# Second-round convolutions one per two steps, and weight sums begun eight steps later, in the up stage of a one-core hybrid block

## The chip, the core and the metric

One core of a Trainium2 chip runs the whole program. The metric is the device time in microseconds of one execution; the number compared is the median of several runs. Engines are called as the profile calls them: PE multiplies matrices (PEld is its weight load), DVE and ACT work elementwise, POOL and SP mostly issue DMAs.

## The reference

A transformer block for 256 tokens of width 2048: three kinds of attention merged by gates, and then a feed-forward part. The change touches only the feed-forward part, which in the reference is

```
h2 = rms_norm(x, g_ffn)
u = causal_depthwise_conv(h2 @ w_up, conv_w, conv_b)      # 3 taps along the tokens
u_gate, u_val = split(u, 2)                               # 5632 columns each
x = x + (silu(u_gate) * u_val) @ w_down
```

All in float32. The kernel gets that precision from cheaper matmuls by splitting each operand into a rounded part (hi) and the rest (lo) and adding the products.

## The kernel before, in words

**Up stage.** The 5632 gate columns and 5632 value columns are cut into 44 tiles of 128 each. The loop over `f0` takes four tiles at a time, first of the gate half (`s` = 0) and then of the value half (`s` = 1). One such pass is called a round here: 11 values of `f0` times two, 22 rounds. The first round is (f0 = 0, s = 0), the second (0, 1), the third (4, 0), the fourth (4, 1). A round goes over the 2048 inputs in 8 **steps** of two k-tiles; 176 steps in all, numbered here from 0, so the second round is steps 8 to 15 and the third 16 to 23.

A step needs 512 KB of `w_up`. `piece` (lines 134 to 146) issues the load on SP, rounds it on ACT into `hi_u` (L141), and subtracts on DVE to get `lo_u` (L142). Then PE runs 8 pairs of matmuls: L1168 multiplies `hi_u` with 512 columns (the tokens' hi and lo parts side by side), L1169 multiplies `lo_u` with the 256 hi columns. There are four buffers each of `raw`, `hi` and `lo`, so a step's operands can be ready a few steps ahead.

**Work beside the matmuls.** After its matmuls each step calls `tick()`, which advances two kinds of generators by one:

- `background` holds two streams of `weight_sums`. Every 8 steps each of them loads a piece of `w_down` (two DMAs of 256 KB on SP, L258), forms sums of its blocks on DVE (L267, L268, L269), and six steps later stores them to DRAM (L272), from where the down stage reads them. `delay` is the number of ticks that a stream waits before its first piece: `14 + 2 * i` here. The staging tiles are `pre_d…`, the stored ones `kept_d…`.
- `later(...)` puts a generator in a queue of which at most two (`WINDOW`) are active. A finished round queues four `conv`: copy and add from PSUM (L1110 on ACT, L1111 on DVE), scale by the row norm `rbc` (L1120 DVE), then three taps (L1125 ACT, L1126 and L1127 DVE). For the gate half follows SiLU (L1129 ACT). For the value half follow the product with the gate (L1133 DVE) and the split of the result into `aT` (L175 ACT, L176 DVE). A `conv` does all of this in one tick.

The first round is special. Its results are ready before `rbc` is: `rbc` is computed from the sum of squares, stored and read back by two POOL DMAs (L1044, L1045). So `first_convs` empties the PSUM banks at once, waits three ticks, and applies one convolution per tick after that.

The loads, the splits of `piece` and the sums keep their order in the program; the convolutions' instructions are placed among them by a scheduler that follows dependencies. Each engine then executes its own list strictly in that order, so an instruction of a convolution that stands ahead of a `lo_u` split on DVE delays that split.

At f0 = 40 the streams must have taken all their pieces; what they have left to issue is drained there.

Of the kernel before, what the change touches and what calls it, by code (L numbers as in the profile page):

```python
# [9 lines left out]
F32 = mybir.dt.float32  # L10
# [5 lines left out]
P = 128  # L16
# [25 lines left out]
def hybrid_block(  # L42
# [54 lines left out]
    def later(gen):  # L97
        waiting.append(gen)
# [57 lines left out]
    def product(x_of, w, nk, n0, n, name):  # L156

        ps = [bank(f"{name}_{t}") for t in range(NT)]
        wv = w.rearrange("(k p) n -> p k n", p=P)
        for k in range(0, nk, 2):  # L160
            a = min(2, nk - k)
            wh, wl = piece(wv[:, k : k + a, n0 : n0 + n], a, n, f"{name}_{k}")
            order = [(j, t) for j in range(a) for t in range(NT)]
            if k + a == nk:
                order.sort(key=lambda jt: jt[1])
            for j, t in order:
                xk = x_of(k + j)
                xs_ = xk[:, t * P : (t + 1) * P], xk[:, S + t * P : S + (t + 1) * P]
                three(ps[t][:, :n], *xs_, (wh[:, j], wl[:, j]), k + j == 0, k + j == nk - 1)
            tick()  # L170
        return ps
# [558 lines left out]
    ps = proj(C_MQ, MEM_W, "mq")  # L730
# [36 lines left out]
    for c in range(3):  # L767
        ps = proj(c * 512, 512, f"f{c}")
# [7 lines left out]
    ps = proj(1536, 512, "f3")  # L776
# [3 lines left out]
    ps = proj(2048, 262, "f4")  # L780
# [74 lines left out]
    for c in range(3):  # L855
        ps = proj(C_SB + c * 512, 512, f"s{c}")
# [51 lines left out]
    ps = proj(C_SB + 1536, 512, "s3")  # L908
# [4 lines left out]
    ps = proj(C_SB + 2048, 256, "s4")  # L913
# [39 lines left out]
    for m in range(2):  # L953
        gate = []
        for b, plan in enumerate(g_plans[m]):
# [40 lines left out]
            if not plan:  # L996
                biases()
                for n in range(2):
                    ps = proj(c0 + n * 512, 512, f"g{n}_{b}")
# [12 lines left out]
        for n in range(2):  # L1012
            acc = gate[branches[0][3]][n]
            for i, (w, k0, nk, b) in enumerate(branches):
                ps = product(lambda k: oT[:, k0 + k], w[0], nk, (2 * m + n) * 512, 512, f"b{2 * m + n}_{b}")
# [61 lines left out]
    ff = ctx.enter_context(tc.tile_pool(name="ff", bufs=1))  # L1077
# [4 lines left out]
    for i in range(2):  # L1082
        background.append(
            weight_sums(
                lambda name, i=i: ff.tile([P, 1024], F32, tag=f"end{i}", bufs=1, name=name), 8, 6, delay=14 + 2 * i
            )
        )

# [20 lines left out]
    def out_of(ps, dst):  # L1109
        nc.scalar.copy(dst, ps[:, S:])  # L1110
        nc.vector.tensor_tensor(dst, dst, ps[:, :S], ALU.add)  # L1111
        return dst
# [4 lines left out]
    def taken(cr, y, f, s):  # L1117
        ct = s * FT + f
        u = pads[f % 2]
        ins = nc.vector.tensor_tensor(u[:, 2:], cr, rbc, ALU.mult)  # L1120
        if y is not None:
            in_order(ins)
        y = y_tile(f, s) if y is None else y
        tap = lambda j: taps[:, j, ct : ct + 1]
        nc.scalar.activation(y, u[:, 2:], AF.Identity, scale=tap(2), bias=tap(3))  # L1125
        nc.vector.scalar_tensor_tensor(y, u[:, 1 : S + 1], tap(1), y, ALU.mult, ALU.add)  # L1126
        nc.vector.scalar_tensor_tensor(y, u[:, 0:S], tap(0), y, ALU.mult, ALU.add)  # L1127
        if s == 0:
            nc.scalar.activation(y, y, AF.Silu)  # L1129
            ys[f] = y  # L1130
        else:
            g = ys.pop(f)
            nc.vector.tensor_tensor(g, g, y, ALU.mult)  # L1133
            split_to(a_pair(f // 2)[:, f % 2], g)

    def conv(ps, f, s):
        taken(out_of(ps, cp.tile([P, S], F32, tag="cr", bufs=2, name=f"cr_{f}_{s}")), None, f, s)
        return
        yield

    def first_convs(ps):
        kept = []
        padded()
        for f in range(4):
            kept.append(out_of(ps[f], y_tile(f, 0)))
            if f % 2:
                yield
        yield 3
        for f in range(4):
            taken(kept[f], kept[f], f, 0)  # L1150
            yield

    for f0 in range(0, FT, 4):
        if f0 == FA:
            assert not halves
            for g in background:
                deque(g, 0)
            background.clear()
        for s in range(2):
            ps = [bank(f"u{f0 + i}_{s}") for i in range(4)]  # L1160
            c0 = s * D_FF + f0 * P
            for k in range(0, KT, 2):
                hi, lo = piece(upv[:, k : k + 2, c0 : c0 + 512], 2, 512, f"u{f0}_{s}_{k}")
                for j in range(2):
                    first, last = k + j == 0, k + j == KT - 1
                    for i in range(4):
                        c = slice(i * P, (i + 1) * P)
                        nc.tensor.matmul(ps[i], lhsT=hi[:, j, c], rhs=hT(k + j), start=first, stop=False)  # L1168
                        nc.tensor.matmul(  # L1169
                            ps[i][:, :S], lhsT=lo[:, j, c], rhs=hT(k + j)[:, :S], start=False, stop=last  # L1170
                        )
                tick()
            if f0 + s == 0:
                later(first_convs(ps))
                continue
            for i in range(4):
                later(conv(ps[i], f0 + i, s))
# [90 lines left out]
```

## Time and profile before

| quantity | value |
|---|---|
| three runs | 1467.82, 1469.42, 1476.87 us |
| median | 1469.42 us |
| the profiled execution's own time | 1476.86 us |
| its span (first to last instruction) | 1475.1 us |
| PE busy | 1469.3 us (100%) |
| DVE busy | 1193.8 us (81%) |
| ACT busy | 839.8 us (57%) |
| matmuls of the up stage, L1168 and L1169 | 2816 |

The profiled execution is the slowest of the three. What lies around its span is 1476.86 − 1475.1 = 1.8 us. A matmul's duration in the rows overlaps with the next one's, so PE's pace has to be read from the distance between two starts and not from a mean duration; "PE busy 100%" only says that there is hardly a moment without a matmul in flight.

### The profile page before, as it was taken

What the parts mean: (1) busy time and instruction counts of PE and PEld (TensorE: products, weight loads), DVE (VectorE), ACT (ScalarE), POOL (GpSimd) and SP (SyncE); (2) the same over time, 40 slices, a digit from 0 to 9 for tenths busy, and PEclk for the clock granted to TensorE, in tenths of its full rate; (3) what the DMA queues carried; (4) which work ended last, traced back from release to release, by engine and by line L of the source; (5) the groups of instructions that cost most, each with busy time, mean ns of one, the idle gap of its engine ahead of it and who ended that gap; (6) DMA issues with size and microseconds to landing.
All of it is one profiled execution on the core that took longest, in us unless ns stands there. A gap on an engine that the chain in (4) does not pass through costs nothing.

```text
span 1475.1 us, 20662 instructions
## 1 busy us (share of the span) xinstructions
PE 1469.3 (100%) x7335; PEld 1240.1 (84%) x7335; DVE 1193.8 (81%) x1816; ACT 839.8 (57%) x1194; POOL 21.8 (1%) x48
## 2 busy tenths in 40 slices
PE   9999999999999999999999999999999999999998
PEld 7888888888888888888888888888888888888887
DVE  5777676777588899897888889888888877997877
ACT  6755454464364455546666656656556555674664
POOL 0000000021000000000000000000000000000000
PEclk9999999999999999999999999999999999999999
DMA  9686787687868576878778999889888866798795
GB/s 299 200 278 193 221 281 215 186 264 226 248 201 275 165 231 204 275 255 277 244 182 274 306 284 286 271 267 288 278 281 282 260 186 199 242 317 269 252 347 213
DMA packets 205606, 369.55 MB, mean 251 GB/s; under 512 B 13578, under 2 KB 82078, under 8 KB 205246
## 3 DMA queue, kind: packets, MB, share of 16 engines
q1 hardware_dynamic: 204094, 365.99, 78.6%
q10 hardware_dynamic: 1328, 2.11, 0.4%
q8 instruction: 57, 0.93, 0.2%
q14 instruction: 47, 0.39, 0.1%
q0 software_dynamic: 80, 0.13, 0.0%
HBM read 335.67 MB, written 32.51 MB: 250 GB/s over the span
## 4 chain that ended last, share of the span: by engine, by line
PE 98%; DVE 1%; ACT 0%; issue 0%; POOL 0%; POOLq 0%; DVEq 0%
PE u L1168 22%; PE u L1169 11%; PE xd L288 4%; PE xd L286 4%; PE xd L287 4%; PE xg L287 3%; PE xg L286 3%; PE xg L288 3%; PE f L288 2%; PE f L287 2%; PE f L286 2%; PE s L286 2%; PE s L288 2%; PE s L287 2%; PE g L286 2%; PE g L288 2%
## 5 line engine op out<-in xcount | busy, mean ns | idle before, releaser
L1168 PE MATMUL u<-hT,hi_u 128*128 128x512 f32 x1232 | 435.6, 398 | 0.0
L1169 PE MATMUL u<-hT,lo_u 128*128 128x256 f32 x1232 | 345.6, 281 | 0.5 <-DVE lo_u L142 0.5
L1168 PEld LDWEIGHTS u<-hT,hi_u 128*128 128x128 f32 x1232 | 231.5, 188 | 57.3
L142 DVE TENSOR_TENSOR lo_u<-raw_u,hi_u 128x1024 fp32r<-128x1024 f32 x176 | 215.3, 1223 | 72.8 <-ACT hi_u L141 70.9
L141 ACT CAST hi_u<-raw_u 128x1024 fp32r<-128x1024 f32 x176 | 184.8, 1051 | 150.2 <-PE u L1168 122.2
L1169 PEld LDWEIGHTS u<-hT,lo_u 128*128 128x128 f32 x1232 | 232.6, 189 | 0.9 <-DVE lo_u L142 0.9
L281 DVE TENSOR_TENSOR lo_d<-raw_d,hi_d 128x1024 fp32r<-128x1024 f32 x88 | 106.8, 1223 | 20.7 <-ACT hi_d L280 18.0
L280 ACT CAST hi_d<-raw_d 128x1024 fp32r<-128x1024 f32 x88 | 92.0, 1054 | 48.0 <-PE xd L287 23.0
L280 ACT CAST hi_g<-raw_g 128x1024 fp32r<-128x1024 f32 (+1 forms) x64 | 61.7, 973 | 37.4 <-PE xg L287 14.2
L281 DVE TENSOR_TENSOR lo_g<-raw_g,hi_g 128x1024 fp32r<-128x1024 f32 (+1 forms) x64 | 71.0, 1119 | 4.3 <-ACT hi_g L280 4.3
L141 ACT CAST hi_f<-raw_f 128x1024 fp32r<-128x1024 f32 (+1 forms) x40 | 38.6, 968 | 51.9 <-PE f L287 47.2
L142 DVE TENSOR_TENSOR lo_f<-raw_f,hi_f 128x1024 fp32r<-128x1024 f32 (+1 forms) x40 | 44.7, 1119 | 27.9 <-ACT hi_f L141 26.0
L286 PE MATMUL xd<-hi_d,aT 128*128 128x512 f32 x170 | 66.2, 389 | 0.0
L288 PE MATMUL xd<-lo_d,aT 128*128 128x512 f32 x170 | 66.2, 389 | 0.0
L287 PE MATMUL xd<-hi_d,aT 128*128 128x512 f32 x170 | 66.1, 389 | 0.0
L142 DVE TENSOR_TENSOR lo_s<-raw_s,hi_s 128x1024 fp32r<-128x1024 f32 (+1 forms) x40 | 44.7, 1117 | 24.9 <-ACT hi_s L141 23.0
L141 ACT CAST hi_s<-raw_s 128x1024 fp32r<-128x1024 f32 (+1 forms) x40 | 38.5, 962 | 43.7 <-PE s L287 27.7
L1168 PE MATMUL u<-hT_rest,hi_u 128*128 128x512 f32 x176 | 63.1, 398 | 0.0
L142 DVE TENSOR_TENSOR lo_g<-raw_g,hi_g 128x1024 fp32r<-128x1024 f32 x32 | 39.3, 1233 | 23.0 <-ACT hi_g L141 22.5
L1125 ACT ACTIVATE y<-u,taps 128x256 f32<-128x256 f32 x88 | 49.6, 597 | 13.8 <-DVE u L1120 13.8
L141 ACT CAST hi_b<-raw_b 128x1024 fp32r<-128x1024 f32 x32 | 33.4, 1053 | 41.1 <-PE b L287 15.9
L141 ACT CAST hi_g<-raw_g 128x1024 fp32r<-128x1024 f32 x32 | 33.6, 1052 | 37.3 <-PE g L287 34.7
(482 smaller groups left out, 3537.8 us busy)
## 6 DMA issues: line engine op xcount, KB each, us to landing
raw_u<-in_w_up_dram SPq DMA_DIRECT2D x176, 512.0 KB, 4.9
raw_g<-in_w_in_dram SPq DMA_DIRECT2D x96, 512.0 KB, 4.5
raw_d<-in_w_down_dram SPq DMA_DIRECT2D x66, 512.0 KB, 5.4
pre_d<-in_w_down_dram SPq DMA_DIRECT2D x88, 256.0 KB, 4.9
kept_d<-pre_d SPq DMA_DIRECT2D x44, 512.0 KB, 5.8
raw_f<-in_w_in_dram SPq DMA_DIRECT2D x32, 512.0 KB, 4.7
raw_s<-in_w_in_dram SPq DMA_DIRECT2D x32, 512.0 KB, 4.1
raw_o<-in_w_out_dram SPq DMA_DIRECT2D x25, 512.0 KB, 5.6
```

Of the source, the lines that this page charges most:

```text
L141: pin(nc.scalar.copy(hi[:, :m], raw[:, :m]))
L142: pin(nc.vector.tensor_tensor(lo[:, :m], raw[:, :m], hi[:, :m].bitcast(F32), ALU.subtract))
L280: nc.scalar.copy(hi[:, :n], src)
L281: nc.vector.tensor_tensor(lo[:, :n], src, hi[:, :n].bitcast(F32), ALU.subtract)
L286: fix(nc.tensor.matmul(o, lhsT=ah, rhs=w[0], start=first, stop=False))
L287: fix(nc.tensor.matmul(o, lhsT=al, rhs=w[0], start=False, stop=False))
L288: fix(nc.tensor.matmul(o, lhsT=ah, rhs=w[1], start=False, stop=last))
L1125: nc.scalar.activation(y, u[:, 2:], AF.Identity, scale=tap(2), bias=tap(3))
L1168: nc.tensor.matmul(ps[i], lhsT=hi[:, j, c], rhs=hT(k + j), start=first, stop=False)
L1169: nc.tensor.matmul(ps[i][:, :S], lhsT=lo[:, j, c], rhs=hT(k + j)[:, :S], start=False, stop=last)
```

## The change

The streams of weight sums in the up stage wait 22 and 24 steps in place of 14 and 16. And the second round's four convolutions are issued by one generator: nothing in its first tick, then one whole convolution (the `deque` runs it to its end), a tick without one, the next convolution, and so on. Before, up to two were issued in one tick.

```diff
-                lambda name, i=i: ff.tile([P, 1024], F32, tag=f"end{i}", bufs=1, name=name), 8, 6, delay=14 + 2 * i
+                lambda name, i=i: ff.tile([P, 1024], F32, tag=f"end{i}", bufs=1, name=name), 8, 6, delay=22 + 2 * i
...
+    def second_convs(ps):
+        yield
+        for f in range(4):
+            deque(conv(ps[f], f, 1), 0)
+            yield 1
...
-            if f0 + s == 0:
-                later(first_convs(ps))
+            if f0 == 0:
+                later((first_convs, second_convs)[s](ps))
                 continue
```

How this moves instructions is seen best on DVE in the third round. In the names, `lo_u4_0_6` is the lo part for f0 = 4, s = 0 and k-tile 6 (step 19; k-tile 2j is the round's step j). `cr_1_1` and `y_1_1` belong to the convolution of tile 1 of the value half, `y_1_0` to that of the gate half. Before, these are the last 12 rows up to and with the split for step 19; between the split for step 18, `lo_u4_0_4`, and the first of them stand two more:

```order
L1120 TENSOR_TENSOR u_0_6980<-cr_0_1_7204,rbc_5953 128x256
L1127 SCALAR_TENSOR_TENSOR y_3_0_7015<-u_1_6982,taps_110,y_3_0_7015 128x256
L1111 TENSOR_TENSOR cr_1_1_7242<-cr_1_1_7242,u1_1_6955 128x256
L1126 SCALAR_TENSOR_TENSOR y_0_1_7208<-u_0_6980,taps_110,y_0_1_7208 128x256
L1120 TENSOR_TENSOR u_1_6982<-cr_1_1_7242,rbc_5953 128x256
L1127 SCALAR_TENSOR_TENSOR y_0_1_7208<-u_0_6980,taps_110,y_0_1_7208 128x256
L1111 TENSOR_TENSOR cr_2_1_7275<-cr_2_1_7275,u2_1_6956 128x256
L1133 TENSOR_TENSOR y_0_0_6984<-y_0_0_6984,y_0_1_7208 128x256
L1126 SCALAR_TENSOR_TENSOR y_1_1_7246<-u_1_6982,taps_110,y_1_1_7246 128x256
L1120 TENSOR_TENSOR u_0_6980<-cr_2_1_7275,rbc_5953 128x256
L1127 SCALAR_TENSOR_TENSOR y_1_1_7246<-u_1_6982,taps_110,y_1_1_7246 128x256
L142 TENSOR_TENSOR lo_u4_0_6_7288<-raw_u4_0_6_7286,hi_u4_0_6_7287 128x1024
```

With the change, these are the rows behind the split for step 18, up to the split for step 20:

```order
L1126 SCALAR_TENSOR_TENSOR y_3_0_7015<-u_1_6982,taps_110,y_3_0_7015 128x256
L1111 TENSOR_TENSOR cr_0_1_7218<-cr_0_1_7218,u0_1_6954 128x256
L1127 SCALAR_TENSOR_TENSOR y_3_0_7015<-u_1_6982,taps_110,y_3_0_7015 128x256
L1120 TENSOR_TENSOR u_0_6980<-cr_0_1_7218,rbc_5953 128x256
L1111 TENSOR_TENSOR cr_1_1_7273<-cr_1_1_7273,u1_1_6955 128x256
L142 TENSOR_TENSOR lo_u4_0_6_7253<-raw_u4_0_6_7251,hi_u4_0_6_7252 128x1024
L1126 SCALAR_TENSOR_TENSOR y_0_1_7222<-u_0_6980,taps_110,y_0_1_7222 128x256
L1120 TENSOR_TENSOR u_1_6982<-cr_1_1_7273,rbc_5953 128x256
L1127 SCALAR_TENSOR_TENSOR y_0_1_7222<-u_0_6980,taps_110,y_0_1_7222 128x256
L1111 TENSOR_TENSOR cr_2_1_7328<-cr_2_1_7328,u2_1_6956 128x256
L1133 TENSOR_TENSOR y_0_0_6984<-y_0_0_6984,y_0_1_7222 128x256
L142 TENSOR_TENSOR lo_u4_0_8_7286<-raw_u4_0_8_7284,hi_u4_0_8_7285 128x1024
```

Thirteen instructions stood between the splits for steps 18 and 19, and eight between those for 19 and 20; now there are five and five, and the rest comes between later splits.

The second place is DVE at the end of the second round, from the split for step 14 to that for step 15. Before:

```order
L142 TENSOR_TENSOR lo_u0_1_12_7108<-raw_u0_1_12_7106,hi_u0_1_12_7107 128x1024
L267 TENSOR_TENSOR pre_d0_4_1_7128<-pre_d0_4_1_7128 128x512
L268 TENSOR_TENSOR pre_d0_4_1_7128<-pre_d0_4_1_7128 128x256
L269 TENSOR_TENSOR pre_d0_4_1_7128<-pre_d0_4_1_7128 128x256
L1120 TENSOR_TENSOR u_0_6980<-y_0_0_6984,rbc_5953 128x256
L142 TENSOR_TENSOR lo_u0_1_14_7141<-raw_u0_1_14_7139,hi_u0_1_14_7140 128x1024
```

With the change:

```order
L142 TENSOR_TENSOR lo_u0_1_12_7108<-raw_u0_1_12_7106,hi_u0_1_12_7107 128x1024
L1120 TENSOR_TENSOR u_0_6980<-y_0_0_6984,rbc_5953 128x256
L1126 SCALAR_TENSOR_TENSOR y_0_0_6984<-u_0_6980,taps_110,y_0_0_6984 128x256
L1127 SCALAR_TENSOR_TENSOR y_0_0_6984<-u_0_6980,taps_110,y_0_0_6984 128x256
L142 TENSOR_TENSOR lo_u0_1_14_7135<-raw_u0_1_14_7133,hi_u0_1_14_7134 128x1024
```

The three sums are gone from here, and the first convolution's product with `rbc`, with both taps that follow it, now stands directly behind the split for step 14 and ahead of the split for step 15.

The third place is SP's list at the other end of the stage, where the streams are drained. With the change:

```order
L258 DMA pre_d1_12_1_11362<-in_w_down_dram 128x2x256 x2
L272 DMA kept_d1_12_11186<-pre_d1_12_0_11187 512x1x256
L140 DMA raw_u36_1_14_11369<-in_w_up_dram 128x2x512
L140 DMA raw_u40_0_0_11396<-in_w_up_dram 128x2x512
L140 DMA raw_u40_0_2_11440<-in_w_up_dram 128x2x512
L140 DMA raw_u40_0_4_11484<-in_w_up_dram 128x2x512
L272 DMA kept_d1_12_11186<-pre_d1_12_1_11362 512x1x256
L140 DMA raw_u40_0_6_11506<-in_w_up_dram 128x2x512
```

Before, the last store stood in front of `raw_u36_1_10`, one round earlier:

```order
L140 DMA raw_u36_1_8_11303<-in_w_up_dram 128x2x512
L272 DMA kept_d1_12_10962<-pre_d1_12_1_11146 512x1x256
L140 DMA raw_u36_1_10_11326<-in_w_up_dram 128x2x512
L140 DMA raw_u36_1_12_11348<-in_w_up_dram 128x2x512
L140 DMA raw_u36_1_14_11370<-in_w_up_dram 128x2x512
```

Everything of the streams has moved by one round, so that the last store, which went out among the loads of the round (36, 1), now stands among those of (40, 0).

## The prediction

> **What bounds the kernel now.** I read the page first, then who PE waited for, then the starts of PE's matmuls in the up stage, and last the DVE rows ahead of the one wait there.
>
> ```profile
> span 1475.1 us, 20662 instructions
> PE 1469.3 (100%) x7335; PEld 1240.1 (84%) x7335; DVE 1193.8 (81%) x1816; ACT 839.8 (57%) x1194; POOL 21.8 (1%) x48
> ...
> PE 98%; DVE 1%; ACT 0%; issue 0%; POOL 0%; POOLq 0%; DVEq 0%
> ```
>
> PE is 98% of the chain that ended last. In PE's list of waits the up stage has one entry:
>
> ```profile
> PE spare L91 <- DVE qscale L487: 1.2, 1, 1.2
> PE u L1169 <- DVE lo_u L142: 0.5, 1, 0.5
> PE r L895 <- DVE ls L891: 0.2, 1, 0.2
> ```
>
> So the change, which moves only DVE, ACT and SP work, can remove one wait, and add others; nothing else of it is on the path. In the timeline of PE the place is this (start, duration, instruction):
>
> ```profile
> 804.63 0.28 PE L1169 MATMUL u<-hT,lo_u 128*128 128x256 f32 x1
> 804.75 0.39 PE L1168 MATMUL u<-hT,hi_u 128*128 128x512 f32 x1
> 805.68 0.39 PE L1169 MATMUL u<-hT,lo_u 128*128 128x256 f32 x1 [0.55 <-DVE lo_u L142]
> 805.91 0.39 PE L1168 MATMUL u<-hT,hi_u 128*128 128x512 f32 x1
> ```
>
> 804.75 is the start of step 20 (third round, k-tile 8). Its `hi_u` is there; its `lo_u` comes 0.7 us too late: the second matmul starts 0.93 us after the first, where 0.23 us is usual.
>
> More is lost behind it. The next rows are the up stage before, at and behind the wait and its last 15 full steps, restricted to L1168 (length, then busy time and count on PE and on PEld, granted clock, DMA share and GB/s), and one row of the down stage with all engines:
>
> ```profile
> 760.38:804.75 44.37, 44.37 (x130) 24.00 (x129) 1.00 0.85 244
> 804.75:808.38 3.63, 2.86 (x10) 1.50 (x9) 1.00 0.43 96
> 808.38:1243.69 435.31, 435.31 (x1234) 231.51 (x1233) 1.00 0.85 268
> 1201.29:1243.69 42.40, 42.40 (x122) 22.55 (x121) 1.00 0.63 186
> ...
> 1250.00:1450.00 200.00, 200.00 (x884) 165.66 (x883) 170.60 (x234) 125.98 (x160) 0.00 (x0) 1.00 0.87 286
> ```
>
> The stretches were cut at starts of L1168, so their true counts are two lower than shown: 128 pairs (16 steps) in the first, 1232 (154 steps) in the third. That is 44.37 / 16 = **2.773 us a step before the wait** and 435.31 / 154 = **2.827 us a step behind it**, 0.0535 us more, through to the end of the stage. The clock is 1.00 in all rows, and in the down stage a matmul of 512 columns starts every 200 / 884 = 0.226 us, as beside the wait (0.23). So it isn't PE's clock. Nor is it the weight sums or the DMA: the last steps have no sums and a DMA share of 0.63, and keep 42.40 / 15 = 2.827 us. The pace behaves like something that PE falls into at an interruption, and keeps. The stage has two more such points:
>
> ```profile
> 747.44 0.39 PE L1168 MATMUL u<-hT,hi_u 128*128 128x512 f32 x1
> ...
> 750.25 0.40 PE L1168 MATMUL u<-hT,hi_u 128*128 128x512 f32 x1
> ...
> 753.08 0.38 PE L195 MATMUL hT<-ident,xres_again 128*128 128x128 f32 x2
> ...
> 757.60 0.39 PE L1168 MATMUL u<-hT,hi_u 128*128 128x512 f32 x1
> ```
>
> Step 0 takes 2.81 us, behind the change of stage; step 3 begins at 757.60, behind the transposes of `hT`, and from there to 804.75 are 17 steps of 2.774. What inside PE sets the pace the profile doesn't show.
>
> **What the change removes.** The wait comes from DVE. These are its rows up to the late split (start, duration):
>
> ```profile
> 794.59 1.22 DVE L142 TENSOR_TENSOR lo_u<-raw_u,hi_u 128x1024 fp32r<-128x1024 f32 x1
> 795.73 0.41 DVE L1111 TENSOR_TENSOR cr<-cr,u 128x256 f32<-128x256 f32 x1
> 796.06 0.48 DVE L1126 SCALAR_TENSOR_TENSOR y<-u,taps,y 128x256 f32<-128x256 f32 x1
> 796.46 0.42 DVE L1120 TENSOR_TENSOR u<-cr,rbc 128x256 f32<-128x256 f32 x1
> ...
> 800.48 1.22 DVE L142 TENSOR_TENSOR lo_u<-raw_u,hi_u 128x1024 fp32r<-128x1024 f32 x1
> 801.61 0.42 DVE L176 TENSOR_TENSOR aT<-y,aT 128x256 fp32r<-128x256 f32 x1
> 801.95 0.41 DVE L1133 TENSOR_TENSOR y<-y,y 128x256 f32<-128x256 f32 x1
> 802.28 0.48 DVE L1126 SCALAR_TENSOR_TENSOR y<-u,taps,y 128x256 f32<-128x256 f32 x1
> ...
> 804.41 1.22 DVE L142 TENSOR_TENSOR lo_u<-raw_u,hi_u 128x1024 fp32r<-128x1024 f32 x1
> ```
>
> From the split of step 18 to that of step 20 are 804.41 − 794.59 = 9.82 us, for two steps that PE does in 5.55. The split of step 18 had ended 3.6 us before PE needed it (795.81; PE needed it 0.23 us after its step began at 804.75 − 2 × 2.773 = 799.20). 3.6 + 5.55 − 9.82 = −0.7 us: the wait.
>
> From the starts, a split takes 1.14 us of DVE, L1126 0.40 and L1127, its like, the same, and L1111, L1120, L1133 and L176 about 0.33. With the new order:
>
> - Step 18 to 19: five instructions, 2 × 0.40 + 3 × 0.33 + 1.14 = 2.93 us.
> - Step 19 to 20: five, 2.93 us.
> - 20 to 21: four, 2.6 us. 21 to 22: four, 2.6 us.
> - 22 to 23: seven, three of them the first weight sums (0.72, 0.46 and 0.35 from the rows below): 4.0 us.
> - 23 to 24: the last two taps, 1.9 us.
>
> Together 17.0 us against six steps of 2.773 = 16.6, and never more than 1.2 us behind on the way. What slack is there at the start? The split of step 14 is the one before the rows that move:
>
> ```profile
> 783.40 1.23 DVE L142 TENSOR_TENSOR lo_u<-raw_u,hi_u 128x1024 fp32r<-128x1024 f32 x1 [0.81 <-ACT hi_u L141]
> 784.54 0.69 DVE L267 TENSOR_TENSOR pre_d<-pre_d 128x512 f32<-128x512 f32 x1
> 785.26 0.43 DVE L268 TENSOR_TENSOR pre_d<-pre_d 128x256 f32<-128x256 f32 x1
> 785.72 0.42 DVE L269 TENSOR_TENSOR pre_d<-pre_d 128x256 f32<-128x256 f32 x1
> 786.07 0.42 DVE L1120 TENSOR_TENSOR u<-y,rbc 128x256 f32<-128x256 f32 x1
> ```
>
> It ends at 784.63 and PE wants it at 788.34 (six steps before 804.75, plus 0.23): 3.7 us. Then come two intervals in which DVE waits for ACT between product and tap, which takes
>
> ```profile
> L1125 ACT ACTIVATE y<-u,taps 128x256 f32<-128x256 f32 x88 | 49.6, 597 | 13.8 <-DVE u L1120 13.8
> ```
>
> so L1120, 0.6 us on ACT, L1126, L1127 and the split, about 3.0 us each as an estimate from these rows, and two short ones of 1.5 and 2.3 us: 9.8 us for four steps of 2.773 = 11.1. So some 5 us of slack at step 18, not below 3 on the way, and about 4 at the lowest behind it, in place of −0.7. **The wait goes**, with some 3 us to spare. A hidden delay, say ACT late for a tap, costs nothing up to that; beyond it each microsecond is a microsecond of PE.
>
> **What it moves.** The weight sums of one round, six DVE instructions of together 3.1 us (twice 0.72 + 0.46 + 0.35) and four DMAs of 256 KB, leave steps 14 to 17 and the same work comes one round later, in all rounds. No DMA is added. Between the second round's end and step 22 SP now issues only `raw_u`, so those come earlier, never later. From step 24 on each round has what every round had before, in the same places of the round; there the splits were ready some microseconds ahead. One of the tightest, from a round with sums, is step 148:
>
> ```profile
> 1162.29 1.23 DVE L142 TENSOR_TENSOR lo_u<-raw_u,hi_u 128x1024 fp32r<-128x1024 f32 x1
> ...
> 1167.37 0.40 PE L1168 MATMUL u<-hT,hi_u 128*128 128x512 f32 x1
> ```
>
> It ends at 1163.52, 3.9 us before PE's step. So I take nothing for the shift itself. Its cover is those 3.9 us; where it was gone, each microsecond that a split is late would be one of PE's, and the slow pace from there on. At f0 = 40 the last store waits for the last sums on DVE, and `raw_u40_0_6` stands behind it on SP. But that load needs a buffer that the split of `u36_1_14` frees, which follows those sums on DVE; the store holds up nothing that wouldn't wait anyway. The fourth convolution frees its PSUM bank about two steps later than before, between the splits for steps 21 and 22; the fourth round wants it at step 24, at least 2 × 2.77 us after that.
>
> **The sum.** From step 20 to the end of the stage before, 804.75 to 1243.69, are 438.94 us for 155 steps. At 2.773 they are 429.8. The difference is **9.1 us**: 0.8 for the wait and 8.3 for 155 times 0.0535. Of the profiled execution's 1476.86 us this leaves 1467.8 us. The other two runs of before, 1467.82 and 1469.42, are where an execution without the slow pace would be; that fits with a split so nearly in time that it was late in one of the three, but no trace of those two is shown. Against the median of 1469.42 the gain is then only 1.6 us, 0.1%. A measurement of this kernel can tell about 1% from no change.
>
> **Rivals.**
>
> 1. *The pace has another cause than the wait.* Then only the 0.8 us goes: 1476.1 for an execution like the profiled one, and 1468.6 against the median. For it: the pace also changed at the transposes, so an interruption may set it either way, and the changed kernel still passes those; entering the slow pace there would mean 168 steps at 2.827 and about 1467.8 + 168 × 0.0535 = 1476.8. Against it: the pace changed within one pair of the wait, and 16 steps of the same code before it were steady. The Trainium skill bears on this in "TensorE: Matmul & The Clock Gate", Part 1 on the clock gate: PE's clock falls back only after an idle window of about 3.4 us, so by that rule a stop of under 1 us costs itself and no more, which is this rival. The granted clock of 1.00 in the rows above agrees that the clock stayed; the pitch changed all the same. I give 0.27.
> 2. *`rbc` comes too late.* This one ends slower. The product with `rbc` now stands directly behind the split of step 14, and the split of step 15 behind it and both its taps:
>
> ```profile
> 774.51 0.57 POOL L1045 DMA_DIRECT2D rbc<-rstd_row  x1 [8.28 <-DMA rstd_row<-scales]
> ...
> rbc<-rstd_row POOLq DMA_DIRECT2D x1, 128.0 KB, 7.2
> ```
>
>    It lands at 774.51 + 7.2 = 781.7, and DVE comes to it at 784.6 or, with fewer DMAs ahead, a little earlier. PE wants the split of step 15 at 791.1; with 1.9 us for product, tap and tap and 1.2 for the split, `rbc` may be up to 6 us later than here before PE stops. Beyond that PE stops at step 15 and the slow pace may hold from there: 161 × 0.0535 = 8.6 us and the stop, 1476.4 and more, up to 1480 with some 3 us of stop. I give 0.08.
> 3. *The change doesn't remove the lateness*, because ACT or a load, not the order on DVE, holds the third round: 1469.4 for the median, as before. The rows above speak against it, DVE having no gap between 794.59 and 805.63. I give 0.05.
>
> **How the numbers follow.** The forecast, no wait and 2.77 us a step, has 0.6 and gives 1467.8, with 1466 to 1469.5 around it, as two of the runs before lie 1.6 us apart. Rival 1 has 0.27 between 1468.6 and 1476.8, rival 2 has 0.08 up to 1480, rival 3 0.05 at 1469.4. The range from 1466 to 1477 leaves out rival 2's upper part and a little below. All cases but mishaps lie within 1% of 1469.42 (1454.7 to 1484.1): 0.95; 0.03 for slower, if a stop like the one of 0.8 us came back in each of the 20 later rounds (16 us); 0.02 for faster, since the whole stage has only these 9 us to give.
>
> **What would show it.** Right: no entry for L1169 in PE's waits; the splits of steps 19 and 20 several microseconds ahead of PE; sixteen-step stretches at 2.77 us a step through to the end of the stage. Wrong: a step pitch of 2.83 with no wait ahead of it (rival 1), a wait of L1169 at step 15 with DVE standing at L1120 (rival 2), or a wait at f0 = 40 with SP standing at the last store.

## The result, and the profile after

| | before | after |
|---|---|---|
| executions measured side by side | 22 | 22 |
| median | 1469.41 us | 1466.93 us |
| lowest to highest | 1466.96 to 1477.38 us | 1466.33 to 1468.31 us |
| mean | 1471.89 us | 1467.05 us |
| the profiled execution | 1476.86 us | 1466.63 us |

The changed kernel is faster by a third of a percent: the ratio after to before is **0.9967, 95% interval 0.9954 to 0.9981**, some 4.8 us of the mean. The medians alone (2.5 us) hide what happens. The executions of the kernel before fall in **two groups** with nothing between them: 12 of 22 at 1466.96 to 1469.42 us and 10 at 1474.82 to 1477.38 us. The changed kernel has only the short one.

Page of the profile after, the span and the engines:

```profile
span 1464.9 us, 20666 instructions
PE 1459.6 (100%) x7335; PEld 1235.3 (84%) x7335; DVE 1192.2 (81%) x1816; ACT 839.0 (57%) x1194; POOL 21.7 (1%) x48
```

Whom PE waited for, all of the list (line, total us, times, longest):

```profile
PE spare L91 <- DVE qscale L487: 1.2, 1, 1.2
PE r L895 <- DVE ls L891: 0.2, 1, 0.2
```

The entry of the up stage is gone. The up stage's pace, in stretches cut at starts of steps and restricted to the matmul of 512 columns, which is now L1174 (L1168 before; L1175 is the one of 256): steps 4 to 19, step 20, steps 21 to 174, and the last 15 of these.

```profile
759.35:803.72 44.37, 44.37 (x129) 24.00 (x129) 1.00 0.79 218
803.72:806.49 2.77, 2.77 (x9) 1.50 (x9) 1.00 0.85 277
806.49:1233.59 427.10, 427.10 (x1234) 231.04 (x1233) 1.00 0.86 274
1192.00:1233.59 41.59, 41.59 (x122) 22.51 (x121) 1.00 0.64 190
```

44.37 / 16 = 2.773, and 427.10 / 154 = **2.773 us a step through to the end**, where the profile before had 2.827 behind its stop. From step 20 to step 175 are 2.77 + 427.10 = 429.87 us. The same stretch took 438.94 us before.

DVE's splits for steps 18, 19 and 20, and the PE rows at the start of step 20:

```profile
792.20 1.22 DVE L142 TENSOR_TENSOR lo_u<-raw_u,hi_u 128x1024 fp32r<-128x1024 f32 x1
...
795.13 1.21 DVE L142 TENSOR_TENSOR lo_u<-raw_u,hi_u 128x1024 fp32r<-128x1024 f32 x1
...
798.06 1.21 DVE L142 TENSOR_TENSOR lo_u<-raw_u,hi_u 128x1024 fp32r<-128x1024 f32 x1
```

```profile
803.72 0.39 PE L1174 MATMUL u<-hT,hi_u 128*128 128x512 f32 x1
803.95 0.27 PE L1175 MATMUL u<-hT,lo_u 128*128 128x256 f32 x1
```

The split that was 0.7 us late ends at 799.27, and the matmul that needs it starts at 803.95: 4.7 us ahead of it.

The two profiled executions differ by 10.23 us: 9.07 us between steps 20 and 175, 1.03 us ahead of the up stage (its first matmul starts at 746.41, before at 747.44), in a part that the change doesn't touch, and 0.1 us behind it. The start of the stage shifts by itself: in two more profiles of the kernel before it lies at 748.01 and 745.59.

### The profile page after: what moved, and what is told of

The parts are those of the page before. It is cut to its first block, busy times and chain, and to the rows that moved or that the text cites. A ratio compares the mean times of both kernels' runs of the same rounds, so it can differ in the third digit from the quotient of the medians.

```text
span 1464.9 us, 20666 instructions
## 1 busy us (share of the span) xinstructions
PE 1459.6 (100%) x7335; PEld 1235.3 (84%) x7335; DVE 1192.2 (81%) x1816; ACT 839.0 (57%) x1194; POOL 21.7 (1%) x48
## 4 chain that ended last, share of the span: by engine, by line
PE 99%; DVE 0%; ACT 0%; POOL 0%; issue 0%; POOLq 0%; DVEq 0%
PE u L1174 22%; PE u L1175 11%; PE xd L288 4%; PE xd L287 4%; PE xd L286 4%; PE xg L286 3%; PE xg L287 3%; PE xg L288 3%; PE f L288 2%; PE f L286 2%; PE f L287 2%; PE s L286 2%; PE s L288 2%; PE s L287 2%; PE g L286 2%; PE b L286 2%
## 5 line engine op out<-in xcount | busy, mean ns | idle before, releaser
L1174 PE MATMUL u<-hT,hi_u 128*128 128x512 f32 x1232 | 428.3, 394 | 0.0
L1175 PE MATMUL u<-hT,lo_u 128*128 128x256 f32 x1232 | 341.4, 277 | 0.0
L1174 PEld LDWEIGHTS u<-hT,hi_u 128*128 128x128 f32 x1232 | 231.0, 188 | 53.6
L1175 PEld LDWEIGHTS u<-hT,lo_u 128*128 128x128 f32 x1232 | 231.3, 188 | 0.0
L1174 PE MATMUL u<-hT_rest,hi_u 128*128 128x512 f32 x176 | 62.0, 394 | 0.0
```

Of the source, the lines that this page charges most:

```text
L1175: nc.tensor.matmul(ps[i][:, :S], lhsT=lo[:, j, c], rhs=hT(k + j)[:, :S], start=False, stop=last)
```

## Experiments

The theory at the outset: a stop of PE in the up stage sets the pace of the matmuls behind it, so that the late split costs little by itself and 8 us by what follows. Its rival: a stop costs only itself, and the pace has a cause of its own. From here on rounds carry numbers from 0, so that round 3 is the fourth, (4, 1), with steps 24 to 31, and round 5 is (8, 1) with steps 40 to 47.

### Each part of the change alone

The delay alone, in the kernel before:

```diff
-..., 8, 6, delay=14 + 2 * i
+..., 8, 6, delay=22 + 2 * i
```

> Only the streams' delay is changed (22 + 2i), the second round's convolutions stay up to two a tick. Worked out from the order of its DVE list: 16 instructions now stand between the splits for steps 19 and 20, 16 x 0.365 + 1.14 = 7.0 us for a step of 2.77, with some 4.8 us of slack at step 19 (as in the changed kernel): 0.6 us of slack are left. Theory 'stop sets the pace': as long as that slack holds no stop, 2.773 us a step and about 1467 us; in the executions in which it doesn't, the 2.827 pace and about 1476. So mostly 1467 with perhaps some at 1475 to 1477. Rival 'a stop costs only itself': all runs within 1 us of 1467 to 1469.

The convolutions alone: the changed kernel with `delay=14 + 2 * i`.

> Only the second round's convolutions are spread, the streams begin at 14 + 2i as before. From its DVE list: five instructions or fewer between any two splits of steps 18 to 22, so with 3.6 us of slack at step 18 (as before) none falls under 3 us. Both theories: no wait of PE in the up stage. 'Stop sets the pace': 2.773 us a step throughout, 1466.9 us like the changed kernel, and no run above 1470. If the weight sums' share matters by itself: above the changed kernel by 0.5 us or more, or some runs at 1475 to 1477.

Measured, 12 executions each: the delay alone 1467.23 us in the median (ratio to before 0.9955, interval 0.9935 to 0.9975), the convolutions alone 1467.62 us (0.9968, 0.9948 to 0.9988). The kernel before had 17 of 29 executions in its long group beside them. Neither profile has a wait in the up stage, and both keep 2.773 us a step: 410.45 / 148 and 410.46 / 148. So either part is enough on most executions. They aren't equally good. In the kernel with the delay alone DVE ends the split of step 20 half a microsecond ahead of PE:

```profile
802.94 1.24 DVE L142 TENSOR_TENSOR lo_u<-raw_u,hi_u 128x1024 fp32r<-128x1024 f32 x1
...
804.45 0.39 PE L1168 MATMUL u<-hT,hi_u 128*128 128x512 f32 x1
804.68 0.27 PE L1169 MATMUL u<-hT,lo_u 128*128 128x256 f32 x1
```

and one of its 12 executions took 1475.61 us. With the convolutions alone that split ends at 799.86, more than 4 us ahead, and none of 12 was above 1469.35 us.

### A stop put into the changed kernel

The split of one step in round 5 (step 42) is made seven times, which changes no value. The splits of that round are also held to the program's order (cut from the diff: the line that the loop replaces):

```diff
+    again = {"u8_1_4": 7}
...
+        for _ in range(again.get(name, 1)):
+            ins = nc.vector.tensor_tensor(lo[:, :m], raw[:, :m], hi[:, :m].bitcast(F32), ALU.subtract)
+            tc.keep_in_program_order(ins) if name.startswith("u8_1_") else pin(ins)
```

> The changed kernel with the split of one step (round (8, 1), k-tile 4: step 42) done seven times over with the same result, so that PE must stop there, by about 2 us (six more splits of 1.2 us against some 6 us of slack). 'Stop sets the pace': 2.773 us a step up to step 42, 2.827 from there to step 175, 133 x 0.0535 = 7.1 us on top of the stop: about 1466.9 + 2 + 7.1 = 1476. 'A stop costs only itself': about 1469, and 2.773 on both sides.

The stop came out longer than meant, PE's list of waits has

```profile
PE u L1179 <- DVE lo_u L145: 9.7, 2, 8.6
```

and the scheduler had put the four matmuls of 512 columns ahead of the four of 256 there. Behind it the pace is 2.773 (steps 56 to 167):

```profile
917.15:1227.76 310.61, 310.61 (x897) 167.55 (x897) 1.00 0.87 279
```

310.61 / 112 = 2.773. So a stop doesn't always set the slow pace. But the ten executions fall in two groups here too, seven at 1478.46 to 1481.89 us and three at 1485.19 to 1486.00, in a kernel whose parent has one group. The 133 steps behind the stop at 0.0535 us more would make 7 us, and the groups' medians lie 5.2 us apart; no execution of the long group has a trace, so this is a hint and no more.

### Eighteen interruptions without a stop

In the changed kernel each of rounds 3 to 20 begins with extra matmuls, whose values the round's own first matmul overwrites. Nothing waits for them.

```diff
+                if k == 0 and (2 * f0 // 4 + s) in breaks:
+                    n, w = breaks[2 * f0 // 4 + s]
+                    for _ in range(n):
+                        nc.tensor.matmul(ps[0][:, :w], lhsT=hi[:, 0, :P], rhs=hT(0)[:, :w], start=True, stop=True)
```

> The changed kernel with extra matmuls at the start of 18 of the later rounds, one kind for each round: 1 to 16 matmuls of 64, 128, 256, 384 or 512 columns that repeat the round's first product (the real one starts the sum anew, so the result is the same). No engine is waited for. 'An interruption sets the pace': some of the rounds run at 2.827 us a step and others at 2.773, by what stood before them; the narrow ones, like the transposes in round 0, should give 2.773, and those of 512 columns, like the end of the stage before, about 2.82. 'Only a stop of PE sets it': all rounds at 2.773. The extra matmuls themselves add about 20 us.

The profiled execution took 1483.06 us and has no wait in the up stage. The pace changed at many of the interruptions, always to one of the two values and never to a third. Two stretches of six steps, in rounds 5 and 6, with the clock at 1.00:

```profile
863.55:880.19 16.64, 16.64 (x49) 8.98 (x49) 1.00 0.86 272
887.57:904.53 16.96, 16.96 (x50) 9.02 (x49) 1.00 0.80 244
```

16.64 / 6 = 2.773 and 16.96 / 6 = 2.827. The whole list (inserted matmuls and their columns at the start of the round, and the pace of its steps behind that):

```
2.827: round 3 1x128   4 2x128   6 16x128   7 1x256   8 2x256   9 4x256
       12 8x512  16 3x512  17 16x128  18 16x256  19 1x64
2.773: round 5 4x128  10 1x512  11 2x512  13 1x384  14 3x128  15 3x256  20 4x64
```

The rule that was expected, 2.773 behind narrow insertions and about 2.82 behind 512 columns, doesn't hold: one and two matmuls of 128 columns stand in the slow row, one and two of 512 in the fast one. Is it chance, then? The same kernel again:

> The kernel with extra matmuls at the start of 18 rounds a second time, unchanged. In its first profile the eight rounds that begin with 1x128, 2x128, 16x128, 1x256, 2x256, 4x256, 8x512, 3x512, 16x128, 16x256 and 1x64 extra matmuls went on at 2.827 us a step and those with 4x128, 1x512, 2x512, 1x384, 3x128, 3x256 and 4x64 at 2.773. If what is inserted decides, the same rounds take the same pace again, and all executions lie within 1 us of 1483. If it is thrown, other rounds are slow this time, and the executions spread by about 2 us each way (18 rounds of 0 or 0.43 us each).

(The expectation counts eight slow rounds and names eleven; eleven it is.) All 18 rounds took the same pace as in the first profile, and the four executions lie at 1483.27 to 1485.49 us. So for matmuls that follow one another without a wait the same sequence of insertions was followed by the same paces, and no chance is left that the two traces show. This holds for the whole sequence: one kind of insertion was not always followed by one pace, as will be seen.

### The kernel before, twice more

> The kernel before once more, for its profile. Its executions so far fall in two groups, 1466.9 to 1470.0 us (12 of 29) and 1474.7 to 1478.0 us (17 of 29). Latched pace: the stop at step 20 (0.7 to 0.9 us) is in every execution; in the long group the steps behind it take 2.827 us, in the short group 2.773 us, so that an execution of 1467 to 1470 us shows the stop and 2.773 behind it. Rival, the stop itself comes and goes: an execution of the short group shows no wait of the matmuls in the up stage at all. Rival, the two groups differ somewhere else: the pace is the same in both, and the 8 us lie in another stage.

> As the run ahead of it, the kernel before a further time: by its time it belongs to one of the two groups, and the same three readings are told apart. Two more profiles show at least one of the short group with a chance of about two in three.

They took 1476.88 and 1465.91 us: one of each group. In the long one, the split of step 20, PE's rows at step 20, and the pace of the 154 steps behind:

```profile
804.45 1.22 DVE L142 TENSOR_TENSOR lo_u<-raw_u,hi_u 128x1024 fp32r<-128x1024 f32 x1
...
805.33 0.39 PE L1168 MATMUL u<-hT,hi_u 128*128 128x512 f32 x1
805.72 0.39 PE L1169 MATMUL u<-hT,lo_u 128*128 128x256 f32 x1
...
808.41:1243.67 435.26, 435.26 (x1233) 231.44 (x1233) 1.00 0.85 267
```

The split ends at 805.67, and the second matmul starts 0.39 us after the first in place of 0.23: the matmul is 0.16 us late, too little to stand in the list of waits. The pace behind is 435.26 / 154 = 2.826 us all the same. In the short execution the same places read

```profile
801.26 1.22 DVE L142 TENSOR_TENSOR lo_u<-raw_u,hi_u 128x1024 fp32r<-128x1024 f32 x1
...
802.90 0.39 PE L1168 MATMUL u<-hT,hi_u 128*128 128x512 f32 x1
803.13 0.27 PE L1169 MATMUL u<-hT,lo_u 128*128 128x256 f32 x1
...
802.90:1213.36 410.46, 410.46 (x1186) 222.01 (x1185) 1.00 0.87 275
```

The split ends at 802.48, 0.65 us ahead of its matmul; 410.46 / 148 = 2.773. So in these three traces the stop itself comes and goes, and with it the pace. It can be followed back to the second round, where ACT waits for a load. The rows of the rounding for step 14, of the profile before, the long and the short execution:

```profile
782.32 1.05 ACT L141 CAST hi_u<-raw_u 128x1024 fp32r<-128x1024 f32 x1 [0.98 <-DMA raw_u<-in_w_up_dram]
```

```profile
782.36 1.05 ACT L141 CAST hi_u<-raw_u 128x1024 fp32r<-128x1024 f32 x1 [0.57 <-DMA raw_u<-in_w_up_dram]
```

```profile
779.17 1.05 ACT L141 CAST hi_u<-raw_u 128x1024 fp32r<-128x1024 f32 x1 [0.50 <-DMA raw_u<-in_w_up_dram]
```

PE begins step 14 six steps of 2.773 us ahead of step 20, at 788.11, 788.69 and 786.26: ACT has the load 5.8, 6.3 and 7.1 us ahead of that. From the split of step 14 to that of step 20 the profile lists no gap of DVE in any of the three, so DVE hands the difference on: the split of step 20 ends 0.65 and 0.11 us later than its matmul would have started (0.23 us behind the start of the step), and 0.65 us ahead of it. The load's margins lie 0.54 and 0.76 us apart, and so do these. Why the load comes sooner or later is not shown.

### Stops of six lengths

Splits at one step of rounds 3, 6, 9, 12, 15 and 18 are repeated 4 to 6 times in the changed kernel.

> The changed kernel with the split of lo_u repeated 4, 4, 5, 5, 6 and 6 times (on the same tile, the values unchanged) at k-tile 4 of rounds 3, 6, 9, 12, 15 and 18, so that the matmuls stop up to six times, about 0 to 8 us each. A stop throws the pace anew: behind each stop the steps take 2.773 or 2.827 us and keep that until the next stop, both values appear, and no third. A stop costs only itself: 2.773 everywhere. The size decides: stops below about 1 us are followed by 2.827, long ones by 2.773 (the one of 8.6 us was). Time: 1467 us, the stops themselves (together 10 to 30 us), and up to 7 us for the pace.

1541.55 us. PE's waits:

```profile
PE u L1179 <- DVE lo_u L145: 61.0, 6, 13.7
```

The pace behind the six stops was 2.773 five times and 2.827 once, behind the fifth (45.22 / 16, against 44.37 / 16 behind the last):

```profile
1160.24:1205.46 45.22, 45.22 (x129) 24.05 (x128) 1.00 0.88 279
...
1244.26:1288.63 44.37, 44.37 (x129) 24.00 (x128) 1.00 0.75 228
```

The first stop is 2.9 us long, the others 11.5, 9.5, 12.6, 10.7 and 13.7. The one of 10.7 us was followed by the slow pace, those of 9.5 and 11.5 by the fast one, so the length doesn't decide. As in the kernel with one stop, the scheduler had reordered the matmuls at these places.

### The late split made certain, and tried to be mended

In the kernel before, the split of step 20 is made twice:

```diff
+    again = {"u4_0_8": 2}
...
+        for _ in range(again.get(name, 1)):
             pin(nc.vector.tensor_tensor(lo[:, :m], raw[:, :m], hi[:, :m].bitcast(F32), ALU.subtract))
```

> The kernel before with the split of lo_u of step 20 made twice (1.2 us more of VectorE ahead of the matmul that is late in about half of its executions). The split is then late in every execution, by some 0.6 to 2.1 us. Latched pace: the steps behind it take 2.827 us to the end of the stage, and all executions, not half of them, lie in one long group: 1466.9 + 0.6 to 2.1 + 8.3 = 1476 to 1477.5 us. A stop costs only itself: 1467.5 to 1469 us. The pace is thrown after each stop, half and half: two groups about 8 us apart.

The median is 1471.87 us, and two groups stay: 7 of 12 executions at 1467.86 to 1472.58 us, 5 at 1477.43 to 1478.82. The profiled one (1468.90 us) belongs to the first group, and shows the longest stop yet in the alternating order with no price at all behind it:

```profile
803.46 0.39 PE L1171 MATMUL u<-hT,hi_u 128*128 128x512 f32 x1
806.00 0.39 PE L1172 MATMUL u<-hT,lo_u 128*128 128x256 f32 x1 [2.15 <-DVE lo_u L145]
...
808.65:1235.75 427.10, 427.10 (x1234) 230.39 (x1233) 1.00 0.85 273
```

427.10 / 154 = 2.773. The theory that any stop sets the slow pace falls. What stands: behind a stop that DVE ends either pace can come. The long group of this kernel has no trace.

To mend the slow pace, one matmul of 512 columns was added at the start of round 3, which with the list above had turned 2.827 into 2.773:

```diff
+                if k == 0 and (f0, s) == (4, 1):
+                    nc.tensor.matmul(ps[0][:, :512], lhsT=hi[:, 0, :P], rhs=hT(0)[:, :512], start=True, stop=True)
```

> The same late split, and one extra matmul of 512 columns (its values are overwritten) at the start of round 3, four steps behind the stop. In two profiles such a matmul turned 2.827 us a step into 2.773. Latched pace: the stop stays and its price goes: 2.773 from round 3 on, 1466.9 + 0.6 to 2.1 + 0.2 + 0.25 = 1468 to 1469.5 us, about 8 us below the kernel with the late split alone. If the late split is dear because it delays the work behind it, or because the following splits stay late, the extra matmul changes nothing but its own 0.23 us: 1476 to 1478 us.

It failed: 10 of 12 executions at 1477.68 to 1481.03 us, 2 at 1469.23 and 1471.33 (the profiled one). None of the ten has a trace, so which pace they had ahead of the inserted matmul isn't known. The profiled one has 2.773 on both sides of the inserted matmul (399.37 / 144 behind it):

```profile
819.22 0.39 PE L1168 MATMUL u<-hT,hi_u 128*128 128x512 f32 x1
819.45 0.40 PE L1173 MATMUL u<-hT,hi_u 128*128 128x512 f32 x1
...
819.45:1218.82 399.37, 399.37 (x1153) 215.36 (x1152) 1.00 0.86 275
```

### The slow pace without any wait

The changed kernel with one extra matmul of 128 columns at the start of round 3, and as a control with one of 512 columns:

> The changed kernel, whose matmuls wait for nothing in the up stage, with one extra matmul of 128 columns at the start of round 3. In two profiles such a matmul turned 2.773 us a step into 2.827. Latched pace: no wait anywhere, and yet 19 rounds of 8 steps at 0.053 us more, 8.1 us: 1466.9 + 0.1 + 8.1 = 1475 us in all executions, slower than the changed kernel by as much as the kernel before is in its long group. If the pace hangs on a late split: 1467.1 us.

> The changed kernel with one extra matmul of 512 columns at the same place, the control of the two runs ahead of it. If what is inserted decides which pace follows, 2.773 us a step stays (2x512 and others left it so; 1x512 was seen only behind 2.827): 1466.9 + 0.25 = 1467.2 us. If any interruption of the even row of matmuls sets 2.827 from 2.773: 1475 us, as with 128 columns.

With 128 columns: 1475.15 us, all 12 executions between 1474.41 and 1476.98. The place, and the pace from step 4 to it and behind it:

```profile
815.25 0.22 PE L1171 MATMUL u<-hT,hi_u 128*128 128x128 f32 x1
815.31 0.44 PE L1176 MATMUL u<-hT,hi_u 128*128 128x512 f32 x1
...
759.77:815.31 55.54, 55.53 (x162) 29.98 (x161) 1.00 0.77 215
815.31:1222.39 407.08, 407.08 (x1152) 216.60 (x1153) 1.00 0.87 275
```

55.54 us are 20 steps of 2.774 and the inserted 0.06; 407.08 / 144 = 2.827. **One matmul of 0.06 us, for which nothing waits, costs 8.2 us.** That is the price of the long group, without a late split: PE's pace alone makes the 8 us that the long executions lose.

The control was no control: the matmul of 512 columns set the slow pace as well, 1475.42 us, 12 of 12 between 1474.41 and 1477.58. Here 1x512 led from 2.773 to 2.827; in the list it led from 2.827 to 2.773; in the kernel with the late split it left 2.773. So the pace ahead and the kind of insertion don't suffice to tell the pace behind. But the pace hides a difference. Rows ahead of the insertion, first of the control, then of the kernel with the late split, both at 2.773 us a step:

```profile
814.67 0.39 PE L1176 MATMUL u<-hT_rest,hi_u 128*128 128x512 f32 x1
814.90 0.27 PE L1177 MATMUL u<-hT_rest,lo_u 128*128 128x256 f32 x1
815.01 0.40 PE L1176 MATMUL u<-hT_rest,hi_u 128*128 128x512 f32 x1
815.24 0.28 PE L1177 MATMUL u<-hT_rest,lo_u 128*128 128x256 f32 x1
```

```profile
818.17 0.39 PE L1173 MATMUL u<-hT_rest,hi_u 128*128 128x512 f32 x1
818.40 0.28 PE L1174 MATMUL u<-hT_rest,lo_u 128*128 128x256 f32 x1
818.52 0.39 PE L1173 MATMUL u<-hT_rest,hi_u 128*128 128x512 f32 x1
818.75 0.28 PE L1174 MATMUL u<-hT_rest,lo_u 128*128 128x256 f32 x1
```

In the control two kinds of pairs take turns; behind the stop of the late split every pair is alike. So 2.773 has two patterns. One matmul of 512 columns was followed by 2.827 from the first, by 2.773 from the second, and by 2.773 from the slow pace. In the kept profiles the same insertion behind the same pattern was never followed by different paces. But only one such case stands in two different kernels (one matmul of 128 columns behind the first pattern, 2.827 both times), so that the pattern decides is a conjecture.

### What lets the row have two paces

The sixteen matmuls of a step alternate between 512 and 256 columns. Two kernels take the alternation away, four of 512 and four of 256 columns, and eight and eight:

```diff
                     for i in range(4):
                         c = slice(i * P, (i + 1) * P)
                         nc.tensor.matmul(ps[i], lhsT=hi[:, j, c], rhs=hT(k + j), start=first, stop=False)
+                    for i in range(4):
+                        c = slice(i * P, (i + 1) * P)
                         nc.tensor.matmul(
                             ps[i][:, :S], lhsT=lo[:, j, c], rhs=hT(k + j)[:, :S], start=False, stop=last
                         )
```

> The changed kernel with the sixteen matmuls of a step in another order: of each k-tile first the four of 512 columns, then the four of 256, where they alternate now. In the rows of the stage a start of 512 columns is followed by one of 256 after 0.230 us, and one of 256 by one of 512 after 0.1167 us; in the stages ahead, 512 follows 512 after 0.2267 us. If the two paces and the 0.3467 us of a pair come from the alternation, a pair falls to 0.2267 and 0.113 to 0.1165, 0.340 to 0.343 us, a step to 2.72 to 2.75, and the kernel to 1466.9 - 176 x (0.03 to 0.05) = 1458 to 1462 us. If the pace is a matter of the weights that are loaded for each matmul or of the count of instructions, it stays at 2.773 or 2.827: 1467 or 1476 us.

> The same with eight of 512 columns and then eight of 256 in each step, so that the width changes twice in a step, where it changes four times in the kernel ahead of it and sixteen times in the changed kernel. If each change of width costs a few ns, the three lie on a line: this kernel saves 14 of the 16 changes, the one ahead 12. If not, it is as long as the one ahead of it within 1 us.

They were to be the faster version, and are not: 1472.61 us (ratio to before 1.0009, 0.9990 to 1.0029) and 1469.94 us (0.9982, 0.9963 to 1.0002), each in one narrow group of 12. Rows of the kernel in fours:

```profile
948.51 1.09 PE L1174 MATMUL u<-hT_rest,hi_u 128*128 128x512 f32 x4
949.44 0.64 PE L1177 MATMUL u<-hT_rest,lo_u 128*128 128x256 f32 x4
949.92 1.09 PE L1174 MATMUL u<-hT,hi_u 128*128 128x512 f32 x4
```

and of the one in eights:

```profile
1137.01 2.00 PE L1173 MATMUL u<-hT,hi_u 128*128 128x512 f32 x8
1138.85 1.12 PE L1177 MATMUL u<-hT,lo_u 128*128 128x256 f32 x8
1139.80 0.40 PE L1173 MATMUL u<-hT,hi_u 128*128 128x512 f32 x1
```

A matmul of 256 columns behind another takes 0.95 / 8 = 0.119 us where I had put 0.113 to 0.1165, and one of 512 takes 1.84 / 8 = 0.230 where I had put 0.227. That is 0.349 us for a pair, and in fours (949.92 − 948.51) / 4 = 0.3525 in these rows, on average 0.351 (415.39 us from step 26 to step 174, 2.807 us a step), against 0.3467 in the alternating order at its better pace. 176 x 0.033 = 5.8 us, about the 5.7 us between 1472.61 and 1466.93. Nor do the three orders lie on a line, as they would if each change of width had a price: from four changes a step to two 2.7 us are saved, from sixteen to four 5.7 are lost.

The kernel before in this order, and the changed one in this order with the inserted matmul of 128 columns:

> The kernel before (whose split of step 20 is late in about half of its executions) with the order four of 512, four of 256. The first matmul of 256 columns of a step comes three starts of 0.227 us later, so a split that was 0.05 to 0.85 us late is late by 0.2 us at most or in time. If the two paces belong to the alternation, the two groups of executions are gone: one group within 3 us, at most 1 us above the changed kernel in the same order. If they don't, the groups stay, some 8 us apart, when the split is still late.

> The changed kernel in the order four of 512, four of 256, with one extra matmul of 128 columns at the start of round 3, which in the alternating order set the pace to 2.827 us a step in all twelve executions (1475 us). If the two paces belong to the alternation: its own 0.1 us and no more, the time of the kernel without it. If they don't: some 8 us more than without it.

1472.87 us (1472.23 to 1474.33) and 1472.69 us (1472.08 to 1474.57), against 1472.61 us without either edit. The inserted matmul costs nothing that can be measured, where in the alternating order it cost 8.2 us, and the kernel before has one group, while the unaltered one beside it still had two (22 of 35 executions up to 1470.37 us, 13 from 1475.38 us on). In that kernel's profile the split of step 20 is in time, so it doesn't test a late split in this order; the inserted matmul does test an interruption, of one kind. **As far as that goes, the two paces belong to the alternation of 512 and 256 columns**, and the alternation at its better pace is the best order tried. No version tried beats the changed kernel.

## Why the prediction was right or wrong, point by point

- **The wait goes, with microseconds to spare.** Right. The estimate was some 5 us at step 18 and about 4 at the lowest behind it; the rows give 5.0 us there (793.42 against 798.17 + 0.23) and 4.7 us at step 20.
- **The pace holds 2.773 us to the end of the stage, 9.1 us less in the profiled execution.** Right: 9.07 us. The predicted 1467.8 us for that execution came out as 1466.63 because 1.03 us were lost ahead of the stage in the one execution and not in the other.
- **Nothing for the shift of the weight sums, none for the drain at f0 = 40, none for the PSUM bank.** Right: the up stage has no wait at all.
- **Rival 1, the pace has another cause than the wait.** Wrong for this change and half right as a mechanism. The one matmul of 128 columns shows that the slow pace needs no wait, and the late split doubled shows that a wait needn't bring it. In the kernel before the late split was the interruption that threw the pace, so taking it away was enough. That the changed kernel enters the stage at the better pace rests on the transposes of `hT`: they were followed by 2.773 in every profile of the alternating order. The prediction took that over from one profile.
- **Rival 2, `rbc` too late, and rival 3, the lateness stays.** Neither came.
- **The step that failed is the last term, the size of the gain against the kernel before: "Against the median of 1469.42 the gain is then only 1.6 us, 0.1%. A measurement of this kernel can tell about 1% from no change."** I had seen that two of three executions of before were without the slow pace and had said that the split was late "in one of the three". The forecast for the changed kernel itself, 1467.8 us, was only 0.9 us above what was measured; what it was compared with was wrong. From the one in three followed that the change is worth the *share* of such executions times 9 us. I took the median of three instead, which for two separate groups is the value of one group and not a size of the gain. Over 22 executions the share was 10: 10/22 x (1476.65 − 1466.93, the median of the long group against that of the changed kernel) = 4.4 us, and 12/22 x (1467.99 − 1466.93) = 0.6 us for the short group, together 5.0 us against 4.8 measured. The other half of the error is the bound of 1%: the changed kernel's 22 executions lie within 2 us, and a difference of 0.33% was told from none with an interval of 0.14% on either side.
- **A slip in the description of the kernel before.** I wrote that the splits of `piece` keep their order in the program. That is so until `pinned[0]` is set to False, ahead of the up stage; there the scheduler places them among the convolutions' instructions as well. The order shown was the built one, so no number hangs on it.

How often the kernel before falls in its long group isn't constant: 10 of 22, 17 of 29, 0 of 7, 16 of 35 and 13 of 35 executions lay above 1474 us in the five comparisons. What the change is worth varies with it, from nearly nothing to some 6 us. Only one short execution of the unaltered kernel has a trace (1465.91 us), and its split was in time; whether others were late and kept the faster pace is open. The executions of 1469 to 1472 us between the groups are unexplained.

## What to carry to other kernels

Where a kernel's executions fall in two groups, a margin of the order of the run-to-run shift is the first suspect: find the instruction that is ready a few tenths of a microsecond before or after it is needed, and work out the gain as the share of long executions times what they lose, not from a median of three. A stop's price can lie behind it: compare the distance between starts ahead of and behind every interruption, not only the list of waits, which did not name the 0.16 us that cost 8.3. And before a long row of matmuls is reordered for an ideal sum of pitches, measure the pitch in that very order: the one worked out from other stages was over 10 us too good.

## What the runs showed of the hardware

**Two paces of one row of matmuls.** Alternating matmuls of 512 and 256 columns, each with its own weights, run at 0.3467 or at 0.3533 us a pair (2.773 or 2.827 us for eight), at a granted clock of 1.00 in both cases, and keep the pace for hundreds of microseconds until the next interruption, be it a stop or one inserted matmul. With inserted matmuls and no wait the pace behind is the same from execution to execution; behind stops that another engine ended both came. What inside PE holds it isn't shown. The Trainium skill, "TensorE: Matmul & The Clock Gate", Part 2, "Back-to-back issue gap", gives 518 and 262 cycles at 2.4 GHz for the isolated gaps of 512 and 256 columns; by that a pair would be 0.325 us as an estimate, and one value. The trace differs in both points, and the measurement decides.

**Which stops touch the clock.** Behind the 2.15 us stop of the late split the granted clock stayed at 1.00. Behind the first of the six stops, 2.94 us, it did not; the row is the stretch around that stop, restricted to the matmul of 512 columns, with the granted clock in the third place from the end:

```profile
822.00:830.00 8.00, 4.71 (x10) 2.60 (x10) 0.79 0.50 130
```

The Trainium skill, same page, Part 1, lets the clock fall after an idle window of about 3.4 us; the trace agrees in kind, with 2.94 us already enough here. The slow pace is another matter: there the granted clock is 1.00.
